# Stores of the recurrent branch's results, issued from GpSimd's queue instead of SyncE's

## The chip, the cores and the metric

The kernel runs on one core of a Trainium2 chip. The metric is the device time of one execution in microseconds (us); where several runs are shown, it is their median. The engines are named as in the profile: PE is TensorE, DVE VectorE, ACT ScalarE, POOL GpSimd, SP SyncE, which computes nothing and only issues transfers. "SPq" and "POOLq" are the instruction queues of SP and POOL where they issue a transfer.

## What is computed

One layer of a decoder with two branches beside each other: a gated linear recurrence (RG-LRU) over the sequence and a chunkwise retention. The sequence is 4096 rows of width 1024, behind 16 learned meta rows. Shortened, with u the normalized input:

```python
proj = jnp.einsum('btd,de->bte', u, w_in[l])
lru_x, lru_gate, q, k, v, ret_gate = jnp.split(proj, split_idx, axis=-1)
xc = _causal_conv(lru_x, conv_w[l], conv_b[l])
y_lru = _rg_lru(xc, w_rg[l], b_rg[l], w_ig[l], b_ig[l], lru_lambda[l]) * jax.nn.silu(lru_gate)
...
y = jnp.concatenate([y_lru, y_ret], axis=-1)
h = h + jnp.einsum('bte,ed->btd', y, w_out[l])
return _rmsnorm(h, final_norm_gain)[:, N_META:]
```

`_rg_lru` computes gates r and i from xc, a decay a = exp(-8 r softplus(-lam)), and the recurrence h = a h + sqrt(1 - a^2) i xc along the sequence.

## The kernel before

The kernel has three stages: the recurrent branch (0 to about 880 us), retention, and a sweep of output products that ends the kernel. `y_lru` goes through device memory in between: the recurrent stage stores it into 32 tensors `ydram[n]` (one for each 128 rows of the sequence), and the sweep loads them again as `yraw` from 2082 us on.

**The recurrent stage** runs two halves of the channels (`ph` 0 and 1), and in each the tiles `i` of the sequence: 272 columns (the 16 meta rows and 256), then 256, then eight of 512. A tile has four blocks `b` of 128 channels. For each block:

- two projections into PSUM, `px` (recurrence input) and `pg` (gate), 24 matmuls each: eight slices of the width, each as three products of high and low halves of the float32 operands (`mm3`, L118 to L120). `px` and `pg` have two PSUM buffers each. The halves of x are `xhi` and `xlo` (`split`, L109 on ACT and L110 on DVE), those of the weights `lwh` and `lwl`.
- `block_front`: `xlb` (L525) is `px` scaled by `rb`, the inverse norm of each row, broadcast to all partitions; three multiply-adds (L531) make the convolution `xc`; it is split into `xch` and `xcl`.
- `block_back`: gate products `pgt` from `xch` and `xcl`; then L548 on DVE writes `sg` = `pg` times `rb`, which frees the `pg` bank; then activations (L549 to L558).
- `tail`, one per block of the tile before: the decay and input (L569, L570), the scan (L571), and L575, which makes the result `sg` in place. L578 stores it: one transfer per 128 columns, 64 KB, so two for a tile of 272 or 256 columns and four for one of 512, 256 in all.

The pool of `sg` has five buffers. L548 of a block therefore writes into the buffer that the block five before it has stored from, and must wait until that store has landed.

**The inverse norm** of the next tile: `xn` is loaded (SP), ACT sums its squares, POOL computes `rstd` (`rsqrt_mean`, L75 and L76). SP stores it as a row `rrow` (L464, 512 elements of 4 bytes) and loads it back broadcast as `rb` (L480). For the next half's weights SP loads `lraw` (L129), POOL multiplies it by a gain (L136), ACT and DVE split it.

**Order.** Every engine runs its own instructions in order. The kernel is built with a scheduler that simulates a time line and sets each engine's order by it (`issue_after` adds some constraints by hand), so an edit of one instruction can move others. In this text "place A" is the stretch 75 to 95 us (tile 1 and the start of tile 2 in half 0) and "place B" 400 to 450 us (from half 0 to half 1).

Of the kernel before, what the change touches and what calls it, by code (L numbers as in the profile page):

```python
# [17 lines left out]
P = 128  # L18
# [15 lines left out]
def hybrid_kernel(ctx: ExitStack, tc: tile.TileContext, xa, x, meta, w_in, w_out,  # L34
                  w_rg, w_ig, vecs, fgain, trig, trigm, mask, dec, ident, out):
    nc = tc.nc
    store = nc.sync
# [10 lines left out]
    ydram = [dpool.tile([P, 8, P], F32, name=f"ydram{n}") for n in range(NT)]  # L48
# [393 lines left out]
    with ExitStack() as ab:  # L442
# [123 lines left out]
        def tail(ph, i, back, T, tiles):  # L566
            b, a, t, m, sg, ex = back
            ch = 4 * ph + b
            nc.vector.scalar_tensor_tensor(t[:, :T], a[:, :T], 1.0, t[:, :T], op0=ALU.add, op1=ALU.mult)  # L569
            nc.vector.tensor_tensor(m[:, :T], m[:, :T], t[:, :T], op=ALU.mult)  # L570
            nc.vector.tensor_tensor_scan(t[:, :T], a[:, :T], m[:, :T],  # L571
                                         0.0 if i == 0 else carry[:, b:b + 1],
                                         op0=ALU.mult, op1=ALU.add)
            nc.vector.tensor_copy(out=carry[:, b:b + 1], in_=t[:, T - 1:T])
            nc.vector.tensor_tensor(sg[:, :T], sg[:, :T], t[:, :T], op=ALU.mult)  # L575
            o = NM if i == 0 else 0
            for j, n in enumerate(tiles):
                store.dma_start(out=ydram[n][:, ch, :], in_=sg[:, o + j * P:o + (j + 1) * P])  # L578

        lw, gws, xparts = {}, {}, {}  # L580

# [19 lines left out]
        def finish(prev, conv=None):  # L601
            nonlocal backs, tails
            ph, gw, st, Tp, pi_, ptiles = prev
            backs.append(block_back(ph, gw, st, Tp))
            if len(backs) == 4:
                tail_roots(backs, Tp)
                tails = [(ph, pi_, bk, Tp, ptiles) for bk in backs]
                backs = []
            if tails and conv is not None:
                with tc.issue_after(conv.ins):  # L610
                    tail(*tails.pop(0))
# [66 lines left out]
        while tails:  # L678
            tail(*tails.pop(0))


    with ExitStack() as cd:
# [25 lines left out]
        for ph in range(2):  # L708
# [180 lines left out]
            for h in range(4):  # L889
                p2, j = divmod(h, 2)  # L890
# [136 lines left out]
```

## Time and profile before

| | us |
|---|---|
| median of 3 runs | 2747.47 |
| lowest and highest | 2746.57, 2751.71 |
| the profiled execution's own time | 2744.62 |
| its span in the trace | 2742.8 |
| PE busy (clock granted, mean of the span) | 2687.7 (0.993) |
| DVE, ACT, POOL busy | 2062.1, 1251.8, 347.8 |
| transfers issued by SP | 418594 packets, 321.44 MB |
| transfers issued by POOL | 13248 packets, 48.24 MB |

The clock is given as a share of TensorE's full speed: 1.00 is 2.4 GHz and 0.50 is 1.2 GHz. The trace gives for every instruction its start, its duration and, in brackets, the idle time before it on its engine and what ended that. Matmuls overlap, so the sum of their durations exceeds their share of the time.

### The profile page before, as it was taken

The page shows a single profiled execution, that of the slowest core. Times are in us where ns is not written, and L with a number is a line of the kernel's source. Part 1 is how long each engine was busy: PE and PEld are TensorE (multiplying, and loading weights), DVE is VectorE, ACT ScalarE, POOL GpSimd, SP SyncE. Part 2 cuts the span into 40 slices and gives each one's busy share as a digit, 9 for nine tenths or more (in the row PEclk, how much of TensorE's full clock was granted, in tenths as well). Part 3 has the DMA queues.
Part 4 walks back from the last instruction along what each step waited for, and adds up shares of the span by engine and source line. Part 5 has one row for each costly group of instructions (what it writes and reads, how often), then busy time and mean ns, then how long its engine had stood idle before and what let it go on. Part 6 is the DMA issues. An engine that isn't in the chain of part 4 may idle for free.

```text
span 2742.8 us, 36798 instructions
## 1 busy us (share of the span) xinstructions
PE 2687.7 (98%) x12934; PEld 2262.3 (82%) x12934; DVE 2062.1 (75%) x4543; ACT 1251.8 (46%) x2297; POOL 347.8 (13%) x634
## 2 busy tenths in 40 slices
PE   7999999999999999999999999999998999999998
PEld 7788888888888888888888888888887888877886
DVE  6688789767679877777779888888778755566665
ACT  5666666554455433333335434443435322244443
POOL 3101021000000111111111111111111101012222
PEclk9999999999999999999999999999999999999999
DMA  6576665432435443434345444445323755476664
GB/s 190 189 236 181 190 185 172 138 127 89 152 100 164 108 99 96 103 93 103 93 103 142 127 119 109 132 130 163 83 66 81 201 114 108 108 206 168 174 159 123
DMA packets 432028, 372.03 MB, mean 136 GB/s; under 512 B 158513, under 2 KB 361810, under 8 KB 431330
## 3 DMA queue, kind: packets, MB, share of 16 engines
q1 hardware_dynamic: 418594, 321.44, 40.0%
q0 software_dynamic: 13248, 48.24, 8.5%
q8 instruction: 101, 1.65, 0.2%
q14 instruction: 85, 0.70, 0.1%
HBM read 254.11 MB, written 132.27 MB: 141 GB/s over the span
## 4 chain that ended last, share of the span: by engine, by line
PE 84%; DVE 6%; DMA 4%; issue 2%; ACT 2%; POOL 1%; SPq 0%; DVEq 0%; POOLq 0%; ACTq 0%
PE ps L119 13%; PE ps L118 13%; PE ps L120 13%; PE pg L118 3%; PE pg L120 3%; PE pg L119 3%; PE px L118 3%; PE px L120 3%; PE px L119 3%; PE po L829 2%; PE oc L308 2%; PE oc L310 2%; PE oc L309 2%; PE od L310 2%; PE od L309 2%
## 5 line engine op out<-in xcount | busy, mean ns | idle before, releaser
L120 PE MATMUL ps<-cwh,xlo 128*128 128x512 f32 x1536 | 599.3, 390 | 0.9 <-DMA xlo<-xs 0.9
L119 PE MATMUL ps<-cwl,xhi 128*128 128x512 f32 x1536 | 599.5, 390 | 0.0
L118 PE MATMUL ps<-cwh,xhi 128*128 128x512 f32 x1536 | 599.3, 390 | 0.0
L120 PEld LDWEIGHTS ps<-cwh,xlo 128*128 128x128 f32 x1536 | 288.3, 188 | 62.5 <-DMA xlo<-xs 1.4
L118 PEld LDWEIGHTS ps<-cwh,xhi 128*128 128x128 f32 x1536 | 288.7, 188 | 57.0 <-issue 0.2
L119 PEld LDWEIGHTS ps<-cwl,xhi 128*128 128x128 f32 x1536 | 288.3, 188 | 56.1 <-issue 0.2
L697 DVE STREAM_TRANSPOSE pT<-rd 32x128 f32<-32x128 f32 x1024 | 310.1, 303 | 16.4
L118 PE MATMUL px<-xhi,lwh 128*128 128x512 f32 (+2 forms) x576 | 214.8, 373 | 6.1 <-DVE xlb L525 4.2
L118 PE MATMUL pg<-xhi,lwh 128*128 128x512 f32 (+2 forms) x576 | 213.1, 370 | 7.7 <-DVE sg L548 7.1
L120 PE MATMUL pg<-xhi,lwl 128*128 128x512 f32 (+2 forms) x576 | 212.5, 369 | 4.6 <-DVE lwl L113 4.6
L119 PE MATMUL px<-xlo,lwh 128*128 128x512 f32 (+2 forms) x576 | 213.4, 371 | 1.0 <-DVE xlo L110 1.0
L120 PE MATMUL px<-xhi,lwl 128*128 128x512 f32 (+2 forms) x576 | 213.8, 371 | 0.6 <-DVE lwl L110 0.6
L119 PE MATMUL pg<-xlo,lwh 128*128 128x512 f32 (+2 forms) x576 | 212.3, 368 | 0.0
L109 ACT ACTIVATE yop<-yraw 128x512 fp32r<-128x512 f32 x192 | 117.7, 628 | 196.4 <-PE od L310 71.4
L110 DVE TENSOR_TENSOR yop<-yraw,yop 128x512 fp32r<-128x512 f32 x192 | 130.5, 687 | 69.0 <-ACT yop L109 66.7
L531 DVE SCALAR_TENSOR_TENSOR xc<-xlb,vec,xc 128x512 f32<-128x512 f32 (+2 forms) x216 | 153.5, 712 | 22.2 <-ACT xc L528 19.0
L856 ACT ACTIVATE on<-po,nb,rs 128x128 f32<-128x128 f32 x256 | 96.3, 457 | 133.1 <-POOL nb L853 133.1
L118 PEld LDWEIGHTS pg<-xhi,lwh 128*128 128x128 f32 x576 | 109.8, 191 | 26.6 <-DVE sg L548 7.9
L118 PEld LDWEIGHTS px<-xhi,lwh 128*128 128x128 f32 x576 | 110.5, 192 | 25.2 <-DVE xlb L525 4.4
L120 PEld LDWEIGHTS pg<-xhi,lwl 128*128 128x128 f32 x576 | 109.6, 190 | 22.4 <-DVE lwl L113 4.8
L797 DVE SCALAR_TENSOR_TENSOR gs<-th,gs 128x512 f32<-128x512 f32 x64 | 44.2, 690 | 111.4 <-ACT gs L796 111.4
L119 PEld LDWEIGHTS px<-xlo,lwh 128*128 128x128 f32 x576 | 110.5, 192 | 20.6 <-DVE xlo L110 2.1
(217 smaller groups left out, 5777.1 us busy)
## 6 DMA issues: line engine op xcount, KB each, us to landing
xhi<-xs SPq DMA_DIRECT2D x92, 512.0 KB, 4.7
xlo<-xs SPq DMA_DIRECT2D x92, 512.0 KB, 5.8
xn<-in_x_dram SPq DMA_DIRECT2D x32, 512.0 KB, 5.6
ydram<-sg SPq DMA_DIRECT2D x256, 64.0 KB, 1.7
hdram<-in_x_dram SPq DMA_DIRECT2D x32, 512.0 KB, 4.2
yret<-yt SPq DMA_DIRECT2D x256, 64.0 KB, 2.2
yraw<-ydram SPq DMA_DIRECT2D x32, 512.0 KB, 3.4
hdram<-h POOLq DMA_DIRECT2D x32, 512.0 KB, 5.4
```

Of the source, the lines that this page charges most:

```text
L109: hi_op[0] = nc.scalar.activation(hi, src, AF.Identity)
L110: return nc.vector.tensor_tensor(lo, src, hi.bitcast(F32), op=ALU.subtract)
L118: nc.tensor.matmul(ps, ah, bh, start=start, stop=False)
L119: nc.tensor.matmul(ps, ah, bl, start=False, stop=False)
L120: nc.tensor.matmul(ps, al, bh, start=False, stop=stop)
L308: nc.tensor.matmul(ps, ah, bh, start=k == 0 and not more, stop=False, skip_group_check=more)
L309: nc.tensor.matmul(ps, ah, bl, start=False, stop=False, skip_group_check=more)
L310: mm = nc.tensor.matmul(ps, al, bh, start=False, stop=k == 3, skip_group_check=more)
L531: conv = nc.vector.scalar_tensor_tensor(xc[:, :T], xl[:, j:j + T], vec[:, 6 + j, ch:ch + 1], xc[:, :T], op0=ALU.mult, op1=ALU.add)
L697: ins = nc.vector.transpose(dst[32 * g:32 * g + 32, :, 32 * q:32 * q + 32], sv[32 * q:32 * q + 32, :, g, :])
L829: nc.tensor.matmul(po[:, h, :], sm[:, h, :], v[:, h * VD:(h + 1) * VD], start=False, stop=(j == 1))
L856: nc.scalar.activation(on[:, h, :], po[:, h, :], AF.Identity, bias=nb[:, h:h + 1], scale=rs[:, h:h + 1])
```

## The change

One line of `tail`. The store of each block's result is issued by POOL instead of SP; source, destination and size stay.

```diff
             o = NM if i == 0 else 0
             for j, n in enumerate(tiles):
-                store.dma_start(out=ydram[n][:, ch, :], in_=sg[:, o + j * P:o + (j + 1) * P])
+                nc.gpsimd.dma_start(out=ydram[n][:, ch, :], in_=sg[:, o + j * P:o + (j + 1) * P])
```

`store` is `nc.sync`, SP. SP's program goes from 978 rows to 713, POOL's from 622 to 852 (a row can hold several equal instructions in sequence). The other engines keep their instructions, and the scheduler gives some of them another order: around 70 to 105 us, 430 to 500 us, 860 to 930 us and 2100 to 2150 us of the trace before.

SP's queue at place A, before (-) and now (+): `sg` is the result, `xn` the input rows of the next tile, `rrow` and `rb` the inverse norm of tile 2.

```order
-L453 DMA xn<-in_x_dram 128x1024
-L578 DMA ydram_72<-sg 128x128
-L578 DMA ydram_73<-sg 128x128
-L453 DMA xn<-in_x_dram 128x1024 x2
-L578 DMA ydram_72<-sg 128x128
-L578 DMA ydram_73<-sg 128x128
+L453 DMA xn<-in_x_dram 128x1024 x3
 L464 DMA rrow_267<-rstd 128x4x1
 L480 DMA rb<-rrow_267 128x512
```

The four stores have left; the others kept their order. POOL's queue there held only the steps of `rstd` before, L75 and L76 in turn. Now:

```order
L75 TENSOR_SCALAR rstd<-ssum 128x1
L578 DMA ydram_72<-sg 128x128
L578 DMA ydram_73<-sg 128x128
L76 TENSOR_TENSOR rstd<-rstd,pm_half 128x1
L75 TENSOR_SCALAR rstd<-ssum 128x1 x2
L578 DMA ydram_72<-sg 128x128
L578 DMA ydram_73<-sg 128x128
L76 TENSOR_TENSOR rstd<-rstd,pm_half 128x1 x2
```

The last steps of `rstd`, which the `rrow` store reads, stand behind the stores of blocks 0 and 1. DVE at place A, where the rows from L548 on have been reordered (`xcl` is the low half of the convolution of two blocks of tile 1):

```order
 L110 TENSOR_TENSOR xcl<-xc,xch 128x256 x2
+L525 TENSOR_TENSOR xlb<-px,rb 128x256
+L526 COPY hist<-xlb 128x3
 L548 TENSOR_TENSOR sg<-pg,rb 128x256
-L525 TENSOR_TENSOR xlb<-px,rb 128x256
-L526 COPY hist<-xlb 128x3
 L550 SCALAR_TENSOR_TENSOR sg<-tg,sg 128x256
 L558 SCALAR_TENSOR_TENSOR m<-m,xc 128x256
 L548 TENSOR_TENSOR sg<-pg,rb 128x256
 L558 SCALAR_TENSOR_TENSOR m<-m,xc 128x256
-L110 TENSOR_TENSOR xlo<-xraw,xhi 128x1024
 L531 SCALAR_TENSOR_TENSOR xc<-xlb,vec,xc 128x256
```

The split `xlo` of tile 2 has moved from the third row behind the second L548 to the eighth: L531, L550, two L531 and L569 now stand ahead of it. POOL's queue at place B, before (each `lraw` is the raw weights of one projection of one block of half 1):

```order
L136 TENSOR_TENSOR lraw_4248<-lraw_4248,vec_168 128x1024
L136 TENSOR_TENSOR lraw_4255<-lraw_4255,vec_168 128x1024
L136 TENSOR_TENSOR lraw_4455<-lraw_4455,vec_168 128x1024
L136 TENSOR_TENSOR lraw_4487<-lraw_4487,vec_168 128x1024
L136 TENSOR_TENSOR lraw_4562<-lraw_4562,vec_168 128x1024
```

and now:

```order
L136 TENSOR_TENSOR lraw_4248<-lraw_4248,vec_168 128x1024
L136 TENSOR_TENSOR lraw_4255<-lraw_4255,vec_168 128x1024
L578 DMA ydram24_96<-sg_3556 128x128
L578 DMA ydram25_97<-sg_3556 128x128
L578 DMA ydram26_98<-sg_3556 128x128
L578 DMA ydram27_99<-sg_3556 128x128
L136 TENSOR_TENSOR lraw_4455<-lraw_4455,vec_168 128x1024
```

Each group of four stores waits for its own L575 and for nothing else but earlier transfers of the queue.

## Rows read from the trace of the kernel before

**Rows 1.** The page's first section: busy time, share of the span, instructions.

```profile
PE 2687.7 (98%) x12934; PEld 2262.3 (82%) x12934; DVE 2062.1 (75%) x4543; ACT 1251.8 (46%) x2297; POOL 347.8 (13%) x634
```

**Rows 2.** 50 us stretches: busy us (count) of each engine, clock, DMA share, GB/s.

```profile
50.00:100.00 50.00, 39.89 (x244) 36.50 (x244) 28.06 (x72) 26.30 (x51) 3.80 (x8) 0.86 0.65 191
...
400.00:450.00 50.00, 45.31 (x220) 38.36 (x218) 46.05 (x62) 30.32 (x42) 12.14 (x6) 0.97 0.52 153
...
500.00:550.00 50.00, 50.00 (x227) 41.41 (x226) 35.12 (x82) 24.01 (x40) 0.00 (x0) 1.00 0.38 139
...
2100.00:2150.00 50.00, 41.56 (x188) 34.17 (x187) 44.50 (x86) 27.06 (x47) 5.79 (x10) 0.93 0.50 153
```

**Rows 3.** Line L578, the store: issue ns min/median/max, one waiter, us to landing.

```profile
L578 SPq DMA_DIRECT2D ydram<-sg x256: 319/430/1203, 74.7 to 879.7; - x128
...
  DVE sg L548: 36.8, 17
...
DMA to landing us min/median/max: 1.6/1.7/10.9
```

**Rows 4.** PE's timeline at place A: start us, us, instruction [idle before <-releaser].

```profile
80.52 0.39 PE L118 MATMUL pg<-xhi,lwh 128*128 128x256 f32 x1 [1.81 <-DVE sg L548]
...
89.13 0.80 PE L118 MATMUL pg<-xhi,lwh 128*128 128x512 f32 x1 [4.08 <-DVE sg L548]
...
93.14 0.63 PE L119 MATMUL px<-xlo,lwh 128*128 128x512 f32 x1
...
94.24 0.40 PE L119 MATMUL px<-xlo,lwh 128*128 128x512 f32 x1
```

**Rows 5.** VectorE's timeline at place A, same columns.

```profile
76.65 0.43 DVE L575 TENSOR_TENSOR sg<-sg,t 128x272 f32<-128x272 f32 x1
...
80.03 0.42 DVE L548 TENSOR_TENSOR sg<-pg,rb 128x256 f32<-128x256 f32 x1 [2.27 <-DMA ydram<-sg]
...
83.01 0.42 DVE L558 SCALAR_TENSOR_TENSOR m<-m,xc 128x256 f32<-128x256 f32 x1 [0.30 <-ACT m L555]
...
88.65 0.42 DVE L548 TENSOR_TENSOR sg<-pg,rb 128x256 f32<-128x256 f32 x1 [5.22 <-DMA ydram<-sg]
...
89.32 1.22 DVE L110 TENSOR_TENSOR xlo<-xraw,xhi 128x1024 fp32r<-128x1024 f32 x1
...
105.25 0.68 DVE L525 TENSOR_TENSOR xlb<-px,rb 128x512 f32<-128x512 f32 x1
```

**Rows 6.** SyncE's queue at place A: start us, us of issuing, DMAs.

```profile
74.75 0.85 SPq L578 DMA_DIRECT2D ydram<-sg  x2
...
77.11 0.99 SPq L578 DMA_DIRECT2D ydram<-sg  x2
...
78.21 0.43 SPq L464 DMA_DIRECT2D rrow<-rstd  x1
...
88.73 0.32 SPq L480 DMA_DIRECT2D rb<-rrow  x1
```

**Rows 7.** Tile `ydram` from 70 to 90 us: landing of its four stores.

```profile
DMA to landing us min/median/max: 4.8/5.4/10.9
```

**Rows 8.** One 2 us stretch within the second gap, columns of rows 2.

```profile
84.00:86.00 2.00, 1.04 (x5) 0.53 (x3) 0.00 (x0) 2.00 (x4) 0.00 (x0) 1.00 0.00 0
```

**Rows 9.** DMA issues: count, KB each, median us to landing.

```profile
rrow<-rstd SPq DMA_DIRECT2D x7, 2.0 KB, 10.5
```

**Rows 10.** Stores that GpSimd issues: lines L359 and L396, and one landing.

```profile
L359 POOL DMA_DIRECT2D hdram<-h x32: 854/863/1095, 2148.8 to 2423.5; - x32
...
L396 POOL DMA_DIRECT2D out_dram<-h x30: 531/550/644, 2477.4 to 2733.7; - x30
...
out_dram<-h POOLq DMA_DIRECT2D x30, 512.0 KB, 5.6
```

**Rows 11.** Place B on PE, and one of SyncE's waits (total, times, longest).

```profile
445.63 1.22 PE L118 MATMUL pgt<-xch,gwh 128*128 128x512 f32 x2 [4.16 <-ACT xch L109]
...
SPq L578 <- DVE sg L575: 207.9, 47, 10.8
```

## The prediction

> **What bounds the kernel now.** I read the page first: TensorE (PE) is busy 98% of the span, every other engine less [rows 1]. A change to the queue of a store can therefore pay only where PE stands idle or runs at the lower clock. The second view is the table of 50 us stretches [rows 2]. The reader is to see that a stretch inside the recurrent stage, 500 to 550 us, has PE busy 50.00 of 50 us at clock 1.00: there the stores cost PE nothing, and taking them off SyncE's queue (SP) can give nothing. Time is lost in 50 to 100 us (39.89 busy, clock 0.86), in 400 to 450 us (45.31, clock 0.97), where channel half 0 ends and half 1 begins, and in 2100 to 2150 us (41.56), where the output sweep starts, long after the last of these stores.
>
> The third view is the line of the store itself [rows 3]: 256 issues of 0.43 us on SP, to landing in 1.7 us in the median but 10.9 at worst; VectorE's L548 waits for them 36.8 us in 17 waits. L548 matters since it writes into an `sg` buffer, five of which go round, so it must wait until the store of the block five before has landed; and it is L548 that frees the PSUM bank `pg` for PE. Only where PE then has nothing else to do does such a wait count. The fourth view, PE's and VectorE's timelines at 75 to 95 us, shows that place [rows 4, 5]. L548 at 80.03 us waited 2.27 us for a store, and PE 1.81 us for it; L548 at 88.65 waited 5.22 us, and PE 4.08. After the second gap PE's 128x512 matmuls last 0.63 us up to the one at 93.14, against 0.40 at 94.24: that is the clock of 1.2 instead of 2.4 GHz after an idle PE.
>
> **What holds those two stores.** The SP timeline [rows 6]: the stores of block 0 are issued from 74.75 on, those of block 1 from 77.11 to 78.10, the `rrow` store follows at 78.21, and `rb`, which reads `rrow`, can go only at 88.73, the moment at which L548 is released too. The four stores landed after 4.8 us at least and 10.9 at most [rows 7], where 1.7 is usual. Yet in 84 to 86 us the DMA engines show a share of 0.00 and 0 GB/s [rows 8]. So the last store does not lack bandwidth. It is reported landed together with the `rrow` store behind it on the same queue, which takes 10.5 us for 2 KB [rows 9]. I read this as: on one queue the small store's completion is held up with the slow neighbour. Nothing shows that directly; it is the inference on which the gain rests.
>
> **The change, part by part.** (1) *Removed from SP*: 256 issues at 0.43 us, 110 us in 880 us, and the order in which loads stood behind stores that wait for L575. SP is not on PE's path in the full stretches [rows 2], so this is worth 0 there.
>
> (2) *Added to GpSimd (POOL)*: 256 issues. The trace has no 64 KB store on this queue; the nearest rows are its 512 KB stores, 0.55 us each without accumulation (L396) and 0.86 with (L359) [rows 10]. I take 0.55, as the new store does not accumulate, and keep 0.86 as the upper end. A tile of 512 columns has 16 stores: 8.8 to 13.8 us of POOL in some 48 us (the stores end at 880 us [rows 3], and that stage has 16 such tiles and four of about half the length). POOL's fullest stretch near, 400 to 450 us, has 12.14 us busy [rows 2], and 12.1 + 13.8 is 26 of 50, so the work fits; the cover is POOL's idle time. Without that cover each issue would cost its 0.55 us on the path.
>
> (3) *Place A*, 75 to 95 us. Block 1's product ends at 76.65 + 0.43 = 77.08 [rows 5]. Two POOL issues take 1.1 to 1.7 us, so the second is out by 78.2 to 78.8. Its landing is unknown: from below 1.7 us (the median of these stores on SP), from above 5.6 (512 KB on POOL's queue) [rows 3, 10]. That gives 79.9 to 84.4. I take 4 us, nearer the upper end, since `xn` loads still run on the same engines, so 82.5. The `rrow` store is issued later now: its last POOL step stands behind block 1's stores in the new order, so it goes at about 80 to 81 instead of 78.21, and is out of the small store's way. L548 cannot run earlier than its place in VectorE's order: in the trace the L558 ahead of it ends at 83.43, 3.4 us after the first L548 [rows 5]. The first one waits for block 0's store, issued from 74.75 on; with two issues of 0.55 us and 4 us of landing that is about 80.0, so the second L548 runs at 83.4. The ends are 81 (VectorE was ready for the first at 80.03 - 2.27 = 77.8, plus 3.4) and 85 (a landing of 5.6 us).
>
> Next to be late is the lower half `xlo` that PE's matmul at 93.14 reads [rows 4]. In the new order VectorE does L548, L558, L531, L550, two more L531 and L569 before that split: six short ones of 0.41 to 0.48 and a pair, 3.0 us together, and 1.22 us for the split itself: 4.2. From 83.4 that is 87.6, and PE is at this matmul at 87.8 instead of 93.14: 5.3 us. If the clock then stays up, as it does at 80.52 after 1.81 us of idling, two more matmuls gain 0.2 each: 0.4. **Sum for place A: 5.7 us**; with the L548 at 85 it is 4.1, at 81 it is 8.1. PE's own work sets a floor near there: 93.14 less the two gaps of 1.81 and 4.08 and less some 2 us for nine matmuls at 0.63 instead of 0.40 is 85.2, so the gain cannot pass 8.3.
>
> (4) *The `rrow` store 2 to 3 us later*: it delays `rb` from 88.73 to about 92; the first product that needs it is VectorE's L525 at 105.25 [rows 5], which leaves 13 us for a load of 256 KB, where one of 512 KB takes 5.6 [rows 10]. Cost 0.
>
> (5) *Place B*, 440 to 446 us. PE waits 4.16 us for `xch` [rows 11], behind a VectorE that is full with splits of the next half's weights. Its order there hardly changes. POOL's six multiplications of weights (L136) in that stretch now stand between groups of four stores, 2.2 to 3.5 us each. I take 0, with 4.2 us gained and 10.8 us lost as ends: the gap itself, and the longest time that SP waited for a product before it could store it [rows 11], which POOL would now wait.
>
> (6) *The sweep*, 2100 us on: no store of this kind is left; the scheduler's few swaps there are put at 0, within 2 us either way.
>
> The profiled execution took 2744.62 us, and 2744.6 - 5.7 is 2738.9. It lies 2.85 below the median of the runs shown, 2747.47, against which a new median will stand, so the forecast is 2741.8, rounded to 2742. Its own range is 2739 to 2744.
>
> **A rule that speaks against it.** The rows above show one store held while the engines idle. The Trainium skill, page "DMA: Bandwidth & Descriptors", section "Issuing engines are not separate DMA queues", says that DMAs of all issuing engines run on the same 16 DMA engines, and that spreading them "will only save the time on the sequencer it takes to initiate the DMA". By it the store would land as late as now, and the result would be that of rival 1. The idle engines at 84 to 86 us speak for a hold-up in the queue rather than in the engines, so I give it the smaller chance.
>
> **Rivals.**
> 1. *Only the issue moves, or the gain is given back.* The block 1 store is reported landed only when `rrow` is, whatever the queue, or the next limiter eats what place A frees. Then L548 still runs near 88, and the time is 2747.5 with 2 us either way. For it: `rrow` is still in flight when the store's data lands, if that takes over 3 us. Against it: `rrow` is now issued after the store by another 2 us. That the change does nothing at all can be left out: the new order shows the 256 stores on POOL.
> 2. *Slower: weights late at place B.* POOL runs in order. A multiplication L136 now stands behind a store that waits for its product, by up to 10.8 us; the weights' split comes later, and PE waits as long, with a lower clock behind the gap, some 2 us as behind the gap at 89 us. With place A's gain kept: 2741.8 + 10.8 + 2 = 2754.6. It ends slower by over 5.5 us from a wait of about 9 us on with place A's gain kept, or of 3.5 if place A brings nothing. For it: every engine but PE is bunched there. Against it: SP waited in the same way before, with the weights' own loads behind it, so the weights were already late by it.
> 3. *More gained.* SP, free of waiting stores, issues the loads of `lraw` earlier; the weights' splits spread out, and the gap of 4.16 us at place B closes with its slow clock of some 2 us: 2741.8 - 6.2 = 2735.6.
>
> **How the numbers follow.** The forecast has 0.48, rival 1 has 0.19, rival 2 has 0.16, rival 3 has 0.17. A measurement of this kernel can tell about 0.2%, 5.5 us, from no change, so the border of "faster" is at 2742.0, inside the forecast's own range: 0.26 of its 0.48 lie below. Faster is 0.26 + 0.17 = 0.43, the same 0.22 + 0.19 = 0.41, slower 0.16. The range runs from rival 3 with the sweep's 2 us, 2733, to rival 2, 2755.
>
> **What would show it.** Right: in 75 to 95 us no wait of PE for L548 over 1 us, the second L548 at 81 to 85 us, stores of block 1 landing within 6 us, the clock in 50 to 100 us above 0.86, and the matmuls beyond 110 us shifted early by 4 to 8 us; POOL's issue at 0.5 to 0.9 us. Wrong: L548 still released at 88 to 91 us together with `rb`; or PE idle for twice the 4.7 us that 400 to 450 us lacks now; or PE idle in a stretch between 110 and 350 us, which would mean that POOL's order is the new bound.

## The result: slower by 0.55%

The changed kernel takes 2762.99 us in the median of 4 runs (2762.85 to 2763.11), the kernel before 2747.02 beside it: a ratio of 1.0055, 95% interval 1.0042 to 1.0068. The forecast was 2742, the range ended at 2755. The kernel before was timed again with each of the four groups of experiments, which ran on three chips, and differs between groups (medians 2747.0, 2748.7, 2754.4, 2753.7 and 2751.7 us), so kernels are compared by their ratio to the kernel before of their own group.

The profiled execution took 2762.85 us, its span is 2761.1. The page's first section and the 50 us stretches, columns as in [rows 1, 2]:

```profile
PE 2699.5 (98%) x12934; PEld 2266.8 (82%) x12934; DVE 2066.5 (75%) x4543; ACT 1247.7 (45%) x2295; POOL 487.8 (18%) x890
```

```profile
50.00:100.00 50.00, 42.49 (x261) 38.55 (x260) 28.87 (x73) 28.50 (x56) 8.73 (x16) 0.90 0.65 195
100.00:150.00 50.00, 46.67 (x197) 36.68 (x196) 32.96 (x64) 29.82 (x47) 7.77 (x14) 0.97 0.55 173
...
200.00:250.00 50.00, 48.39 (x211) 39.13 (x211) 37.77 (x62) 29.96 (x46) 13.98 (x24) 1.00 0.55 185
...
500.00:550.00 50.00, 49.41 (x296) 43.61 (x295) 35.54 (x94) 27.48 (x53) 8.53 (x16) 1.00 0.46 158
```

Before, 200 to 250 us, like the two stretches on either side of it:

```profile
200.00:250.00 50.00, 50.00 (x221) 41.12 (x220) 38.85 (x65) 31.68 (x47) 5.76 (x8) 1.00 0.64 198
```

Place A did gain (42.49 for 39.89, clock 0.90 for 0.86). The loss sits where nothing was expected: in the tiles of half 0 behind place A, 100 to 410 us, where PE had no gap but one of 0.28 us and now has one or more around each change from one full tile (512 columns) to the next. To see what each place costs in all, gaps and slow clock together, I set the start of PE's n-th matmul after against that of the n-th before (those of lines L118 to L120 and L308 to L310, 12324 in both traces):

```
start before, us   95.6  128.6  162.8  197.0  265.5  299.7  368.1  403.0  436.8  507.2  877.7  2613.3
after - before     -2.7   -2.7   +3.6   +5.8   +8.0  +12.5  +13.7  +20.0  +19.1  +20.3  +20.3   +19.3
```

Place A brings 2.7 us; the tiles of half 0 behind it, 128 to 403 us, cost 22.7; place B, 403 to 507 us, costs nothing; half 1 and all behind it neither, but for 1 us gained in between.

### The profile page after: what moved, and what is told of

Same layout as the page of the kernel before. It is cut to its first block, busy times and chain, and to the rows that moved or that the text cites. A ratio compares the mean times of both kernels' runs of the same rounds, so it can differ in the third digit from the quotient of the medians.

```text
span 2761.1 us, 36839 instructions
## 1 busy us (share of the span) xinstructions
PE 2699.5 (98%) x12934; PEld 2266.8 (82%) x12934; DVE 2066.5 (75%) x4543; ACT 1247.7 (45%) x2295; POOL 487.8 (18%) x890
## 4 chain that ended last, share of the span: by engine, by line
PE 77%; DVE 7%; DMA 7%; ACT 4%; issue 3%; POOL 2%; SPq 0%; DVEq 0%; POOLq 0%; ACTq 0%
PE ps L119 12%; PE ps L118 12%; PE ps L120 12%; DMA ydram<-sg 3%; PE pg L120 2%; PE pg L118 2%; PE px L120 2%; PE px L119 2%; PE pg L119 2%; PE px L118 2%; PE po L829 2%; PE oc L308 2%; PE oc L309 2%; PE oc L310 2%; PE od L309 2%
## 5 line engine op out<-in xcount | busy, mean ns | idle before, releaser
L118 PE MATMUL ps<-cwh,xhi 128*128 128x512 f32 x1536 | 599.3, 390 | 0.0
L120 PE MATMUL ps<-cwh,xlo 128*128 128x512 f32 x1536 | 599.2, 390 | 0.0
L120 PEld LDWEIGHTS ps<-cwh,xlo 128*128 128x128 f32 x1536 | 288.4, 188 | 61.1
L118 PEld LDWEIGHTS ps<-cwh,xhi 128*128 128x128 f32 x1536 | 288.8, 188 | 56.8 <-issue 0.2
L578 POOL DMA_DIRECT2D ydram<-sg x256 | 137.3, 542 | 576.0 <-DVE sg L575 421.4
L118 PE MATMUL px<-xhi,lwh 128*128 128x512 f32 (+2 forms) x576 | 216.9, 377 | 12.9 <-ACT xhi L109 8.6
L118 PE MATMUL pg<-xhi,lwh 128*128 128x512 f32 (+2 forms) x576 | 214.2, 372 | 5.8 <-DVE sg L548 4.7
L120 PE MATMUL pg<-xhi,lwl 128*128 128x512 f32 (+2 forms) x576 | 213.9, 371 | 3.2 <-DVE lwl L113 3.2
L120 PE MATMUL px<-xhi,lwl 128*128 128x512 f32 (+2 forms) x576 | 215.2, 374 | 1.4 <-DVE lwl L110 1.4
L531 DVE SCALAR_TENSOR_TENSOR xc<-xlb,vec,xc 128x512 f32<-128x512 f32 (+2 forms) x216 | 155.5, 721 | 19.2 <-ACT xc L528 16.0
L118 PEld LDWEIGHTS px<-xhi,lwh 128*128 128x128 f32 x576 | 111.2, 193 | 35.4 <-ACT xhi L109 12.2
L118 PEld LDWEIGHTS pg<-xhi,lwh 128*128 128x128 f32 x576 | 110.8, 192 | 25.1 <-DVE sg L548 6.3
L120 PEld LDWEIGHTS pg<-xhi,lwl 128*128 128x128 f32 x576 | 110.8, 192 | 21.7 <-DVE lwl L113 4.0
```

The costliest lines, as they stand in the source:

```text
L118: nc.tensor.matmul(ps, ah, bh, start=start, stop=False)
L120: nc.tensor.matmul(ps, al, bh, start=False, stop=stop)
L531: conv = nc.vector.scalar_tensor_tensor(xc[:, :T], xl[:, j:j + T], vec[:, 6 + j, ch:ch + 1], xc[:, :T], op0=ALU.mult, op1=ALU.add)
L578: nc.gpsimd.dma_start(out=ydram[n][:, ch, :], in_=sg[:, o + j * P:o + (j + 1) * P])
```

## One tile of half 0, before and after

The loss has a fixed shape. These rows show the same tile in both traces. Before, POOL's last `rstd` step, SP's queue, the landing of the four stores issued from 217.18 on, and VectorE's L548:

```profile
215.76 0.92 POOL L76 TENSOR_TENSOR rstd<-rstd,pm_half 128x1 f32<-128x1 f32 x1
```

```profile
216.71 0.38 SPq L464 DMA_DIRECT2D rrow<-rstd  x1
217.18 1.90 SPq L578 DMA_DIRECT2D ydram<-sg  x4
227.32 0.32 SPq L480 DMA_DIRECT2D rb<-rrow  x1
```

```profile
L578 SPq DMA_DIRECT2D ydram<-sg x4: 423/432/464, 217.2 to 218.6; - x4
...
DMA to landing us min/median/max: 9.3/9.6/10.3
```

```profile
228.06 0.69 DVE L548 TENSOR_TENSOR sg<-pg,rb 128x512 f32<-128x512 f32 x1 [4.18 <-DMA ydram<-sg]
```

After, in the same order of views:

```profile
219.34 2.12 POOL L578 DMA_DIRECT2D ydram<-sg  x4 [13.20 <-DVE hist L526]
221.53 3.10 POOL L75 TENSOR_SCALAR rstd<-ssum 128x1 f32<-128x1 f32 x4
224.72 2.58 POOL L76 TENSOR_TENSOR rstd<-rstd,pm_half 128x1 f32<-128x1 f32 x4
227.25 2.21 POOL L578 DMA_DIRECT2D ydram<-sg  x4
```

```profile
227.32 0.38 SPq L464 DMA_DIRECT2D rrow<-rstd  x1
237.57 0.33 SPq L480 DMA_DIRECT2D rb<-rrow  x1
```

```profile
L578 POOL DMA_DIRECT2D ydram<-sg x4: 537/537/612, 227.3 to 228.9; - x4
...
DMA to landing us min/median/max: 9.8/10.3/10.9
```

```profile
224.57 0.68 DVE L575 TENSOR_TENSOR sg<-sg,t 128x512 f32<-128x512 f32 x1
...
238.88 0.69 DVE L548 TENSOR_TENSOR sg<-pg,rb 128x512 f32<-128x512 f32 x1 [6.06 <-DMA ydram<-sg]
```

ScalarE and PE behind it:

```profile
243.25 0.82 ACT L528 ACTIVATE xc<-xlb,vec 128x512 f32<-128x512 f32 x1 [2.31 <-DVE xlb L525]
243.97 2.94 ACT L109 ACTIVATE xhi<-xraw 128x1024 fp32r<-128x1024 f32 x3
```

```profile
245.06 0.50 PE L118 MATMUL px<-xhi,lwh 128*128 128x512 f32 x1 [1.04 <-ACT xhi L109]
...
246.83 0.50 PE L119 MATMUL px<-xlo,lwh 128*128 128x512 f32 x1 [0.57 <-DVE xlo L110]
```

What the reader is to see: in both kernels the stores that run beside the `rrow` store land after about 10 us, when `rrow` does, although after the change they are on POOL's queue and `rrow` is on SP's. So the hold-up is not one of the queue. After the change POOL does two groups of stores and the eight `rstd` steps one behind the other: the product of the second block is ready at 225.25 (224.57 + 0.68), and its stores go at 227.25, with `rrow` at the same moment. From the product's end to L548 it is 13.6 us (238.88 - 225.25); before it was 11.1 (228.06 less 216.93, where the same L575 ended, which started at 216.25). PE does not wait for L548 itself: ScalarE, in order, has the `xhi` of the next tile behind L528, which waits for VectorE's work behind L548.

How much PE had to spare can be counted in its own matmuls, whose order from 150 to 403 us is the same in both traces. Counted as above, L548 starts behind the 1036th of them before and behind the 1059th after. At 0.23 us from one to the next, that is some 5.3 us later in PE's work: 2.5 us between the product's end and L548, the rest already ahead of the product. 1.6 us of it became gaps, so this tile had some 3.7 us to spare.

The line of the store over the whole span, with [rows 3]: the issue is 0.54 us, as POOL's other stores suggested, and L548's wait grew from 36.8 to 44.9 us in total.

```profile
L578 POOL DMA_DIRECT2D ydram<-sg x256: 537/537/802, 75.3 to 900.2; - x128
...
  DVE sg L548: 44.9, 15
...
DMA to landing us min/median/max: 1.9/3.5/12.3
```

## The experiments

Theory A: the meeting of these stores, POOL's `rstd` steps and the `rrow` store makes the loss. In its form A1, the cause is that a store in flight beside `rrow` is told landed only with it; in its form A2, it is the time that POOL's queue takes ahead of the stores and `rrow`. Theory B: a store from POOL's queue lands later everywhere. Theory C: the scheduler's new order on ScalarE and VectorE. "PE busy" below is that of 150 to 400 us, five full tiles of half 0; it was 249.72 of 250 before and is 241.60 after (the second row is half 1):

```profile
150.00:400.00 250.00, 241.60 (x1043) 195.85 (x1042) 186.05 (x302) 148.51 (x219) 71.30 (x116) 0.99 0.56 182
500.00:900.00 400.00, 399.42 (x1843) 331.76 (x1842) 296.75 (x547) 203.47 (x312) 70.75 (x133) 1.00 0.38 130
```

| kernel | median us | ratio to before (95%) | PE busy |
|---|---|---|---|
| stores on POOL in half 0 only | 2760.86 | 1.0058 (1.0042 to 1.0074) | 244.27 |
| stores on POOL in half 1 only | 2745.98 | 0.9996 (0.9987 to 1.0006) | 248.16 |
| after, `rstd` in one pair | 2747.01 | 0.9998 (0.9988 to 1.0007) | 250.00 |
| before, `rstd` in one pair | 2749.60 | 1.0006 (0.9996 to 1.0017) | 248.01 |
| after, quick `rrow` store | 2738.93 | 0.9942 (0.9927 to 0.9957) | 250.00 |
| before, quick `rrow` store | 2738.74 | 0.9947 (0.9932 to 0.9961) | 250.00 |
| after, six `sg` buffers | 2735.81 | 0.9936 (0.9921 to 0.9950) | 250.00 |
| before, six `sg` buffers | 2739.72 | 0.9948 (0.9932 to 0.9965) | 250.00 |
| after, `rrow` held back | 2753.33 | 1.0006 (0.9995 to 1.0018) | 250.00 |
| before, `rrow` held back | 2744.92 | 0.9979 (0.9970 to 0.9988) | 250.00 |
| after, six buffers and one pair | 2734.47 | 0.9941 (0.9926 to 0.9955) | 250.00 |

**Half by half.** The stores of one half on POOL, those of the other on SP:

```diff
-                store.dma_start(out=ydram[n][:, ch, :], in_=sg[:, o + j * P:o + (j + 1) * P])
+                (nc.gpsimd if ph == 0 else store).dma_start(out=ydram[n][:, ch, :], in_=sg[:, o + j * P:o + (j + 1) * P])
```

> Only the stores of half 0 are issued from GpSimd, those of half 1 stay on SyncE. Half 0 is the only one in which the rrow store runs (half 1 reads the same rows again). Theory A (the loss comes from the meeting of these stores, GpSimd's rstd steps and the rrow store): all of the loss is here, 2763 us, with PE idle 1 to 2.6 us once per tile between 100 and 410 us. Theory B (a store from GpSimd's queue simply lands later, 3.5 us against 1.7 in the median, and L548 waits for it everywhere): about half of the loss, 2755 us.

> Only the stores of half 1 are issued from GpSimd. Theory A: no loss, 2747 us within 3, PE without a gap from 500 to 900 us. Theory B: the other half of the loss, 2755 us.

All of the loss is in half 0 (1.0058), none in half 1 (0.9996), where the same 128 stores go from the same queue. Theory B falls: half 1 would have lost as much. What half 0 has and half 1 has not is `rstd` and `rrow`, but also the splits `xhi` and `xlo` that PE waits for in the tile above; half 1 loads these. This pair of runs therefore finds the place, and the next ones the cause.

**The `rstd` steps in one pair.** The eight POOL instructions of a tile become two:

```diff
-                rsqrt_mean(rstd[:, n:n + 1], ssum[:, n:n + 1], P, 1, 1.0 / D)
+                if i == 0:
+                    rsqrt_mean(rstd[:, n:n + 1], ssum[:, n:n + 1], P, 1, 1.0 / D)
...
             if i > 0:
+                rsqrt_mean(rstd[:, tiles[0]:tiles[-1] + 1], ssum[:, tiles[0]:tiles[-1] + 1], P, len(tiles), 1.0 / D)
                 store.dma_start(out=rrow[i][0, :T].rearrange("(n p) -> p n", p=P),
```

> The changed kernel, but GpSimd computes the inverse norm of a tile's four row groups in one pair of instructions (128x4) instead of four pairs (128x1). In the changed kernel the four pairs take 5.7 us and stand between the stores of two blocks. Theory A (the length of that chain on GpSimd delays rrow and the next store): the chain is about 1.5 us, rrow leaves some 4 us earlier, L548 is released as much earlier in every tile of half 0, and most of the loss goes: 2745 to 2750 us. Theory B (later landing on GpSimd's queue): the landing stays, 2760 to 2763. Theory C (the scheduler's new order on ScalarE and VectorE): it would stay near 2763 unless the order changes back.

> The kernel before, stores on SyncE, with the same one pair for the inverse norm: the control of af_batch. Theory A: in the kernel before GpSimd holds nothing but these steps, rrow leaves 2 to 3 us earlier, PE had no gap in those tiles anyway: 2747 us, or up to 5 less if the two gaps at 80 and 85 us shrink as well. Theories B and C: 2747 us.

The stores stay on POOL and the loss against the kernel before is gone (0.9998), PE is full from 150 to 400 us; the same edit brings the kernel before nothing (1.0006). By the comparison of matmuls above, 6.4 us are still lost here between 129 and 163 us, from the first full tile to the second, and nothing from there to 368 us. POOL's timeline in the tile:

```profile
215.36 2.13 POOL L580 DMA_DIRECT2D ydram<-sg  x4 [13.76 <-DVE hist L528]
218.65 0.19 POOL L75 TENSOR_SCALAR rstd<-ssum 128x4 f32<-128x4 f32 x1 [1.15 <-ACT xn L454]
218.92 1.94 POOL L76 TENSOR_TENSOR rstd<-rstd,pm_half 128x4 f32<-128x4 f32 x1
221.56 2.23 POOL L580 DMA_DIRECT2D ydram<-sg  x4 [0.70 <-DVE sg L577]
```

The pair takes 2.2 us instead of 5.7, and POOL now waits for the product at 221.56 instead of the product for POOL. The stores still land after 8.7 to 9.7 us. So the length of the chain on POOL is needed for the loss behind 163 us, but this run alone doesn't tell A1 from A2: both `rrow` and the stores left earlier.

**The hold-up taken away.** From tile 2 on, the `rrow` store of 512 separate elements is replaced by one of a single 2 KB row of a constant:

```diff
+        rfix = tp.tile([1, TB], F32, name="rfix")
+        nc.vector.memset(rfix, 0.03)
...
-            if i > 0:
+            if i > 1:
+                nc.gpsimd.tensor_copy(out=rfix[:, 0:1], in_=rstd[0:1, tiles[-1]:tiles[-1] + 1])
+                store.dma_start(out=rrow[i][:, :T], in_=rfix[:, :T])
+            elif i > 0:
...
```

> The changed kernel, but from tile 2 on the rrow store of 512 elements of 4 bytes is replaced by a store of one 2 KB row of a constant (it still waits for the tile's last rstd step). Left out: the true inverse norms of tiles 2 to 9 in rb. Theory A1 (every store of results that is in flight while the rrow store runs is told landed only when rrow is, on either queue): the stores that took 10 to 11 us land in 2 to 6, L548 has no wait over 2 us from tile 3 on, and PE has no gap from 150 to 400 us: 2740 to 2748 us. Theory A2 (only the order on GpSimd delays, the landing is GpSimd's own slow one): these stores still take 8 us or more, 2755 to 2763.

> The kernel before with the same replaced rrow store (left out: the true inverse norms of tiles 2 to 9). Theory A1: L548's wait of 4.1 us in every tile of half 0 goes, but PE had no gap there, so at most the gaps at 80 and 89 us go: 2740 to 2747. If the time falls below 2738, the wait did cost something that I do not see.

POOL's order in the tile is that of the changed kernel, stores behind the whole `rstd` chain (213.78, straight behind it), and yet:

```profile
211.25 2.58 POOL L76 TENSOR_TENSOR rstd<-rstd,pm_half 128x1 f32<-128x1 f32 x4
213.78 2.21 POOL L583 DMA_DIRECT2D ydram<-sg  x4
```

```profile
L583 POOL DMA_DIRECT2D ydram<-sg x4: 537/538/612, 213.8 to 215.5; - x4
...
DMA to landing us min/median/max: 1.9/1.9/1.9
```

The stores land after 1.9 us, and with no hold-up the two queues are equal: 0.9942 and 0.9947. Theory C falls too. The change did reorder VectorE and ScalarE in the tiles of half 0, beyond the stretches named under "The change" (in the tile above, the L548 ahead of the one shown has moved behind L558). But from 105 to 430 us this kernel's VectorE, ScalarE and PE have the same instructions in the same order as the changed kernel's, and it loses nothing there. The same holds for the kernels with one pair and with `rrow` held back. Here `rrow` also leaves behind the stores, so its size and its moment changed together; the next run holds its size.

**`rrow` held back.** Four more POOL instructions (rstd times one, plus zero) behind each tile's last step, eight in the kernel before:

```diff
             if i > 0:
+                for _ in range(4):
+                    nc.gpsimd.tensor_scalar(rstd[:, tiles[0]:tiles[-1] + 1], rstd[:, tiles[0]:tiles[-1] + 1], 1.0, 0.0, op0=ALU.mult, op1=ALU.add)
                 store.dma_start(out=rrow[i][0, :T].rearrange("(n p) -> p n", p=P),
```

> The changed kernel with four more GpSimd instructions on rstd (times one, plus zero) behind each tile's last step, so that rrow leaves later. In the order that follows, the stores of the next block keep their place behind the four rstd pairs and now stand ahead of the four new instructions: they are issued as late as in the changed kernel, but some 3 us ahead of rrow instead of with it. Theory A1 (the loss is the landing that is held until rrow has landed): the stores land in 2 to 6 us, L548's waits of 6 to 7 us and PE's gaps from 150 to 400 us go, and the time falls to 2740 to 2750 although GpSimd does more and rb is later. Theory A2 (the loss is the time that GpSimd's queue takes before the stores and rrow): nothing gets better, 2763 or more.

> The kernel before with eight such instructions behind each tile's last rstd step. The order puts the stores of the next block ahead of rrow on SyncE's queue, where they stood behind it. Theory A1: the store issued some microseconds ahead of rrow lands in about 2 us, L548's wait of 4 us per tile goes, PE had no gap there: 2738 to 2747 us. If a later rrow itself costs PE (through rb), 2755 or more.

The tile on POOL's timeline, the `rrow` store on SP's, and the landing of the stores issued from 228.43 on:

```profile
225.90 2.58 POOL L76 TENSOR_TENSOR rstd<-rstd,pm_half 128x1 f32<-128x1 f32 x4
228.43 2.21 POOL L580 DMA_DIRECT2D ydram<-sg  x4
230.66 2.16 POOL L465 TENSOR_SCALAR rstd<-rstd 128x4 f32<-128x4 f32 x4
```

```profile
232.85 0.38 SPq L466 DMA_DIRECT2D rrow<-rstd  x1
```

```profile
L580 POOL DMA_DIRECT2D ydram<-sg x4: 537/538/612, 228.4 to 230.1; - x4
...
DMA to landing us min/median/max: 1.9/1.9/1.9
```

This is the run that tells A1 from A2. POOL has more to do, the `rstd` chain still stands ahead of the stores, which go 2.0 us behind their product as in the changed kernel, `rrow` and `rb` are later, and PE has no gap left from 150 to 400 us: the store that runs 4.4 us ahead of `rrow` lands in 1.9 us where it took 10. A2 falls for the full tiles from 150 us on. The total, 2753.33, lies above the expected 2740 to 2750; it is that of the kernel before (1.0006), which is slower in this group. By the comparison of matmuls this kernel is 3.4 us ahead at 110 us, 9.5 us behind at 163 us, and loses nothing from there to 368 us. In between, from the first full tile to the second, the stores were not ahead: those issued from 123.35 to 125.25, beside `rrow` at 124.43, still landed after 9.2 to 10.9 us. In the kernel before, where the order had put the stores behind `rrow`, holding `rrow` back gains 0.2% (0.9979). Being some microseconds ahead did not always do there: in one tile the four stores issued from 272.83 to 274.2, with `rrow` at 276.01, landed after 12.2 to 12.5 us, and L548 waited 5.99 us. PE had no gap behind it, since that L548 stood only 3 matmuls later in PE's work than in the kernel before: the length of a wait does not tell what it costs.

**Six buffers.** `sg` gets a sixth buffer, so that L548 needs the store of one block earlier:

```diff
-            sg = tp.tile([P, TB], F32, tag="sg", name="sg", bufs=5)
+            sg = tp.tile([P, TB], F32, tag="sg", name="sg", bufs=6)
```

> The changed kernel with six sg buffers instead of five, so that L548 waits for the store of the block six before, one block earlier. Theory A1 (the loss passes from the held store to PE only through L548's wait for its buffer): no wait of L548 over 1 us, PE without a gap from 150 to 400 us, and the gaps at place A gone or halved: 2738 to 2748. If instead the late rb (rrow leaves 2 to 3 us later) or the scheduler's order made the gaps, the time stays at 2755 or more.

> The kernel before with six sg buffers. Theory A1: the waits of 4 us per tile in L548 go without a gain, since PE had no gap behind them; the two gaps of 1.81 and 4.08 us at place A and their slow clock go: 2739 to 2744 us.

> Six sg buffers and one pair of GpSimd instructions for the inverse norm, stores on GpSimd: both remedies together. By theory A1 six buffers alone had taken all of the loss in the full tiles, so the pair adds nothing beyond 2 us: 0.992 to 0.996 of the kernel before.

L548's wait was the only path from the held store to PE in these tiles, as far as these runs show it (the sixth buffer also changes VectorE's order there): the stores are held as before (here those issued from 217.58 on, beside `rrow` at 217.65), but no L548 waits for them, PE is full, and both kernels are faster than the one before, the one with the stores on POOL at 0.9936, that with the stores on SP at 0.9948; the intervals overlap, so which queue is better then stays open. The pair of `rstd` steps adds nothing to six buffers (0.9941), as expected.

```profile
L578 POOL DMA_DIRECT2D ydram<-sg x4: 537/537/612, 217.6 to 219.3; - x4
...
DMA to landing us min/median/max: 10.8/11.2/11.8
```

In VectorE's waits from 150 to 400 us, ahead the changed kernel and behind it the changed kernel with six buffers, the row is gone:

```profile
DVE sg L548 <- DMA ydram<-sg: 35.7, 10, 7.3
```

```profile
DVE sg L550 <- ACT tg L549: 2.2, 5, 0.4
DVE sg L548 <- PE pg L120: 0.7, 1, 0.7
```

Six buffers and stores on POOL beat both the kernel before and the changed one, by 0.64% and, by the ratios, by some 1.2%.

**The kernel before once more.** The quick `rrow` store and the six buffers gained 14 to 16 us on the kernel before where its trace explains 6 (spans of 2736.5 and 2737.4 against 2742.8), and three of these four kernels came out 1 to 2 us below the range expected of them. So the kernel before, unchanged, was traced a second time.

> The kernel before itself, for a second trace. The two kernels with a quick rrow store and with six buffers fell further below it (some 14 us) than the first trace explains (some 6 us), and the kernel before stands at 2754 in those groups instead of 2747. If L548's wait has no slack left, a run at 2750 or more shows gaps of PE in the full tiles of half 0 (249.72 of 250 us busy from 150 to 400 us in the first trace, 244 to 248 then), and L548's waits longer than 4.3 us. If the slower time has another place, PE stays at 249.7 there.

It took 2752.58 us in the median, its profiled execution 2749.08. PE's stretch from 150 to 400 us, VectorE's waits there, and PE's gaps there:

```profile
150.00:400.00 250.00, 246.68 (x1079) 201.83 (x1078) 195.20 (x316) 158.58 (x231) 32.58 (x42) 1.00 0.64 190
```

```profile
DVE sg L548 <- DMA ydram<-sg: 25.8, 7, 5.2
```

```profile
339.88 0.50 PE L119 MATMUL px<-xlo,lwh 128*128 128x512 f32 x1 [0.57 <-DVE xlo L110]
...
390.75 0.50 PE L118 MATMUL px<-xhi,lwh 128*128 128x512 f32 x1 [2.17 <-ACT xhi L109]
...
392.51 0.50 PE L119 MATMUL px<-xlo,lwh 128*128 128x512 f32 x1 [0.58 <-DVE xlo L110]
```

L548 waits up to 5.2 us instead of 4.3. In three of the five tiles that costs nothing; in the other two PE has the changed kernel's gaps, for `xhi` and `xlo`, where the first trace had none and one of 0.28 us. In the last of the five L548 stands behind the 1712th matmul instead of the 1700th, some 2.7 us later in PE's work, and the gaps are 2.75 us: that tile has nothing to spare. Two more traces with the stores of half 0 on SP show gaps at the same place, those of the stores on POOL in half 1 only and of the kernel before with one pair (248.16 and 248.01 of 250). So the first trace, from which the prediction was made, was the fullest of the four.

This explains part of the kernel's scatter, and part of why cutting the chain gains more than the first trace showed: the second trace's span is 4.5 us longer than the first one's, and by the comparison of matmuls 3.7 us are lost between 300 and 403 us. The rest of the 8 to 10 us is not shown: the slower executions were not traced, and the group with the quick store and the six buffers ran on another chip, where no trace of the kernel before was taken.

## Why the prediction was wrong, step by step

**What bounds the kernel: the step that failed.** From a stretch with PE busy 50.00 of 50 I concluded that "there the stores cost PE nothing, and taking them off SyncE's queue (SP) can give nothing". The stretch it was read from, 500 to 550 us, lies in half 1, where no `rrow` store runs. In half 0 PE's row looked as full in the first trace, but moving the stores there was not free: the sum has 0 for the tiles of half 0 behind place A, and they cost 22.7 us. L548 waited 4.18 us in the tile before, and the trace of before has 18.0 us of such waits from 150 to 400 us. A wait that is hidden looks in PE's row like one that doesn't exist, and its slack had to be asked: some 3.7 us in the tile shown, of which the change took 5.3, and nothing in the last of the five tiles, as the second trace of the kernel before shows.

**What holds the stores: half right.** That they are held until `rrow` has landed, with the engines idle, was right, and carries the whole result. That the hold is of one queue, "on which the gain rests", was wrong: after the change the stores are held across queues (10.3 us in the median of the tile's four, `rrow` 10.2). The runs with a quick `rrow` store and with `rrow` held back show that it is the slow `rrow` store, and not the queue. Rival 1 had this condition, "whatever the queue", but not the price: it counted place A alone and gave 2747.5. The rule that spoke against the change bore this out, if not in its words: the Trainium skill, "DMA: Bandwidth & Descriptors", section "Issuing engines are not separate DMA queues", says that all issuing engines' transfers run on the same engines, and I gave it the smaller chance. The landing stayed late, as by that rule; the time was not that of rival 1. The same page, section "Queues, rings and completion order", says that the write that reports a completion lands only after earlier writes of that DMA engine, across its queues. The traces agree in their outcome; what happens inside an engine no run here shows.

**Part (4), the later `rrow` store, cost 0: mis-sized.** I counted only who reads `rb` (13 us of slack, and indeed no VectorE wait for `rb` in a full tile). Whoever is held by `rrow` was not counted: with the store and `rrow` leaving together 2 us behind the product, the tiles of half 0 cost those 22.7 us, gaps and slow clock together, the whole of the loss and more.

**Part (2), POOL's issues: right in size, wrong in order.** 0.54 us each against 0.55, and POOL had room (13.98 of 50 us busy). The sum asked whether POOL has time, not what stands in front: the eight `rstd` steps between two groups of stores. Each half has seven full tiles, not eight (272 + 256 + 7 x 512 columns); they last 49 us in the trace, so the 48 us of the sum stand.

**Part (3), place A: right in direction, half in size.** PE waits 2.42 and 0.41 us there now [rows 4], the second L548 is at 86.86 instead of 88.65 [rows 5], and 2.7 us are gained instead of 5.7:

```profile
82.49 0.38 PE L118 MATMUL pg<-xhi,lwh 128*128 128x256 f32 x1 [2.42 <-DVE sg L548]
87.34 0.50 PE L118 MATMUL pg<-xhi,lwh 128*128 128x512 f32 x1 [0.41 <-DVE sg L548]
```

The term that was off is the landing, 4.4 to 8.1 us where 4 was taken (with [rows 7]); the step "out of the small store's way" failed, for `rrow` left at 80.32, as foreseen, and block 1's last store, issued 1.7 us ahead of it at 78.66, still took 8.1 us:

```profile
80.32 0.38 SPq L464 DMA_DIRECT2D rrow<-rstd  x1
```

**Place B and the sweep: right.** Nothing net from 403 to 507 us, although POOL waits up to 13.0 us there for a product; PE's gap at the place of [rows 11] is 2.83 us. Rival 2 had the sign of the result and the wrong place: its mechanism, POOL in order behind a waiting store, acts on `rstd` in every tile of half 0 and not on the weights. "PE idle in a stretch between 110 and 350 us, which would mean that POOL's order is the new bound" is what came, though with POOL's order as the first half of the cause only: the experiments put the other half in the landing.

## What to carry to other kernels

A wait off the busiest engine that shows no gap there may have no slack left: before moving anything in front of it, ask how much later it may end, and count that in the busiest engine's own instructions, not from the busy share or from the length of the wait. When work moves to another engine's queue, list what that queue already holds at that moment, and who waits for those entries. If a buffer's reuse waits for a transfer, one more buffer can be worth more than the choice of the queue: here it gained 0.5 to 0.6% with the stores on either queue.

## What was not expected of the hardware

A 2 KB store of 512 separate elements took 10.2 to 11.5 us to land in the full tiles before and 7.0 to 11.2 after, and 64 KB stores beside it, on either queue, landed about when it did, with the engines at a share of 0.00 [rows 8, 9]. In half 1, where that store does not run, the median was 1.7 us from SP's queue and 1.9 from POOL's. With the slow small store leaving 4.4 us behind the stores instead of beside them, and more work on the way, the loss in the full tiles from 150 us on was gone.
